# Seven block products for eight in the MLP of the last 1,024 tokens, taken together, with attention moved into the first two passes

## The chip, the cores and the metric

One core of one Trainium2 chip. Times are device microseconds of one execution; lower is better. The kernel runs in one launch and uses TensorE (PE), VectorE (DVE), ScalarE (ACT), GpSimd (POOL) and the DMA queue of SyncE (SP).

## The reference, cut to what matters

```python
h = h + concat([att, conv]) @ w_out            # att: dilated windows; conv: conformer
sc = (rmsnorm(h, norm_x_g) @ w_xq) . xk / 16   # cross-attention, 4 heads, 256 keys
h = h + (softmax(sc) . xv) @ w_xo
u = rmsnorm(h, norm_mlp_g) @ w_up              # 1024 -> 4096
h = h + square(relu(u)) @ w_down               # 4096 -> 1024
return rmsnorm(h, norm_final_g)                # 2,048 tokens, width 1,024, float32
```

## The kernel before

The activations lie transposed: a tile is 128 channels by 512 tokens, and width 1,024 is eight such tiles (`KC` = 8). Every large product is made of three matmuls (`mm3`, L197 to L200), since each operand is split into a high part and what the high part leaves over: weight high x activation high (L198), weight high x activation low (L199), weight low x activation high (L200). A weight tile comes as a raw 512 KB tile by a DMA from SP, ACT casts the high part (L189) and DVE subtracts it for the low part (L190); both are in `wsplit2`, and `wpost` (L1088) loads and splits a tile for the passes below.

The first 700 us or so make the queries, keys and values, the first block's attention and the convolution's input. Then come four passes, `post(p)` (L1217), each of 512 tokens: the output projection (tiles `o`, weights `raw_o`), scores and softmax of the cross-attention (`xs`, weights `raw_a`), its projection (`x`, weights `raw_b`), each with a residual and a sum of squares in `resid_linear` (L1194), then the norm's factor for each token, `rsb`, and the MLP. The MLP has eight groups (`fg`) of 512 hidden channels: four times 24 matmuls into one bank (`up`, weights `raw_u`), then relu times `rsb` (L1306), square (L1307), and the split into `hh` high (L1308) and low (L1309); then eight times 12 matmuls (`dn`, weights `raw_d`), each added to the residual `h` by DVE (L1324). So the up product works on activations without `rsb`, which comes in behind it at L1306. At the end the final norm and 16 transposed tiles of rows (`ot`, L1352 to L1356) go out. In the last pass the down products of the last group and the final norm are done for 256 tokens at a time.

The attention and the convolution of block p+1 run beside pass p. They are generators which `weave` (L92) advances by a rate each time the pass yields; what is left is drained at the end of the pass:

```python
sides = [(att(p + 1), 0.95), (conv(cv, p + 1), 0.6)] if p + 1 < NG else []
weave(main, *sides)
drain(*(g for g, _ in sides))
```

The last pass has nothing beside it. The order in which an engine gets its instructions is set by the order of these generators and by a scheduler that moves instructions of one engine past each other when it builds the program; tiles of one tag share a ring of buffers (`bufs`), and a load into a buffer waits for the last reader of what it held before.

Of the kernel before, what the change touches and what calls it, by code (L numbers as in the profile page):

```python
# [10 lines left out]
F32 = mybir.dt.float32  # L11
# [32 lines left out]
def f(ap):  # L44
    return ap.bitcast(F32)


def hybrid_layer(ctx, tc, A, out):
# [722 lines left out]
    early.close()  # L771


    kq = pool("att_keys", side="right")
    aq = pool("att_q", side="right")
    mask = pool("mask", side="right").tile([P, 6 * 256 + P], F32, name="mask")
    dma(mask, A["masks"])
    wk = pool("att_work", side="right")
    wk.tile([P, 144], F32, name="wpad")


# [356 lines left out]


    banks.update(mm=(0, 1, 2), O=(7,))  # L1140
    wq = pool("w_post", side="right")
    xp_ = pool("post_x")
    zp = pool("post_z")
    yp = pool("post_y")
    pp = pool("post")
    cv = pool("conv")
# [4 lines left out]
    def xquad(q, i, name):  # L1151
        return xp_.tile([P, 4, 512], F32R, tag=f"x{q}{i}", name=name)
# [22 lines left out]
        rstd_col(r[:, 0:n], pc[:, 0:n], n, top)  # L1175
        return r

    def load_cat(p, half):

        d = cats.setdefault(p, {})  # L1180
        for q in "hl":
            t = xquad(q, half, f"cat{q}{p}{half}")
# [11 lines left out]
    def resid_linear(load, rhs, korder, resid, hs, ssum, key, y, name, steps=False):  # L1194


        for ms in ((0, 1, 2), (3,), (4,), (5,), (6,), (7,)):
            wt = [load(m) for m in ms]
            pts = {}
            for ks in (korder[0:4], korder[4:6], korder[6:8]) if len(ms) > 1 else (korder,):  # L1200
                for m, (wh, wl) in zip(ms, wt):
                    if m not in pts:
                        pts[m] = ps("mm", f"{name}{m}")
                    for k in ks:
                        mm3(pts[m], wh[:, k, :], wl[:, k, :], rhs["h", k], rhs["l", k], k == korder[0], k == korder[-1])
                    if steps and ks[-1] != korder[-1]:
                        yield
                    if ks[-1] == korder[-1]:
                        h = hs[m]
                        last["dve"] = DVE.tensor_tensor(h, pts[m], resid(m), op=ALU.add)  # L1210
                        ACT.activation(y["h", m], h, AF.Copy, scale=gain(key, m))
                        DVE.scalar_tensor_tensor(y["l", m], h, gain(key, m), f(y["h", m]), op0=ALU.mult,
                                                 op1=ALU.subtract)
                        add_sq(h, ssum, m == 0)
                        yield

    def post(p):  # L1217
        ts = slice(512 * p, 512 * (p + 1))
        if p == 0:
            load_cat(0, 0)  # L1220
            load_cat(0, 1)
        hs = [zp.tile([P, 512], F32, tag=f"z{m}", name=f"h{p}_{m}") for m in range(KC)]

        def ytiles(name):
            return {(q, k): ytile(q, k, f"{name}{q}{p}_{k}") for k in range(KC) for q in "hl"}

        def from_x(m):
            x = tmp("res")
            dma(x, xscr[m][:, ts])
            return x  # L1230

        y = ytiles("y")
        ssum = ssum_tile(f"o{p}")
        yield from resid_linear(lambda m: wout[m] if p == 0 and m in wout else wpost(wcols(w_out, m * P), f"o{p}{m}"),
                                cats[p], [4, 5, 6, 7, 0, 1, 2, 3], from_x, hs, ssum, "x", y, f"o{p}_",
# [43 lines left out]
                        yield  # L1279
                yield  # L1280

        y = ytiles("m")
# [5 lines left out]
        rsb = ssum  # L1288
        ACT.copy(rsb, rb)


        FG = 8
        end = p == NG - 1
        for fg in range(FG):
            hh = {}
            for q in "hl":
# [13 lines left out]
                yield  # L1310
            if fg == FG - 1:
                fsum = ssum_tile(f"f{p}")
                if not end:
                    load_cat(p + 1, 0)

            def down(mp2, t, w, wh, wl):
                sl = slice(t, t + w)
                for e in range(2):
                    m = 2 * mp2 + e
                    es = slice(P * e, P * e + P)  # L1320
                    pt = ps("mm", "dn")[:, 0:w]
                    for k in range(4):
                        mm3(pt, wh[:, k, es], wl[:, k, es], hh["h", k][:, sl], hh["l", k][:, sl], k == 0, k == 3)
                    last["dve"] = DVE.tensor_tensor(hs[m][:, sl], hs[m][:, sl], pt, op=ALU.add)  # L1324
                    if fg == FG - 1:
                        add_sq(hs[m][:, sl], fsum[:, sl], m == 0)

            wd = []
            for mp2 in range(4):
                wd.append(wpost(wcols(w_down, mp2 * 256, 256, (4 * fg, 4 * fg + 4)), f"d{p}{fg}_{mp2}", (P, 4, 256)))  # L1330
                if fg == FG - 1 and end:
                    continue
                down(mp2, 0, 512, *wd[-1])
                yield


        fin = {}

        def final(t, w):
            r = rstd_from(fsum[:, t:t + w])  # L1340
            sl = slice(t, t + w)
            for k in range(KC):
                if t == 0:
                    fin[k] = ytile("h", k, f"fin{p}_{k}", F32)
                DVE.tensor_scalar(fin[k][:, sl], hs[k][:, sl], gain("final", k), None, op0=ALU.mult)
            for j in range(w // P):
                c0 = t + P * j
                for g in range(2):
                    ot = ytile("l", 2 * (c0 // P) + g, f"ot{p}{c0}{g}", F32)
                    pt = ps("T", "ot")  # L1350
                    for i in range(4):
                        PE.transpose(pt[:, P * i:P * i + P], fin[4 * g + i][:, c0:c0 + P], ident)  # L1352
                    if g:
                        ACT.activation(ot, pt, AF.Copy, scale=r[:, j:j + 1])
                    else:
                        DVE.tensor_scalar(ot, pt, r[:, j:j + 1], None, op0=ALU.mult)  # L1356
                    dma(out[0, 512 * p + c0:512 * p + c0 + P, 512 * g:512 * (g + 1)], ot)
                yield

        if end:  # L1360
            for t in range(0, 512, 256):
                for mp2 in range(4):
                    down(mp2, t, 256, *wd[mp2])
                yield from final(t, 256)
        else:
# [12 lines left out]

def _constants():
# [55 lines left out]
```

## Time and profile before

| | |
|---|---|
| three timed runs | 2896.39, 2896.18, 2894.63 us |
| median | 2896.18 us |
| the profiled execution | 2900.79 us, of it 2899.0 between the first and the last instruction |
| mean granted TensorE clock | 0.989 |
| matmul instructions on PE | 15,628 |
| moved by DMA | 433.73 MB |

In the profile's lines an instruction is named by its line, engine, operation and tiles (out<-in, buffer numbers left out). The windows give, for each stretch, the busy time of each engine with the number of instructions, then the granted clock of TensorE, the share of the 16 DMA engines that was busy, and GB/s. Pieces of the chain of waits are: start, duration, what. Pass 1 starts at some 1300 us, pass 2 at 1850, pass 3 at 2400, and the MLP of pass 3 at 2541.

### The profile page before, as it was taken

The numbers are of one execution on the slowest core, as the hardware profiler recorded it, in microseconds if no ns is written. First come the engines' busy times: TensorE is split into PE (matmuls) and PEld (weight loads), VectorE is DVE, ScalarE is ACT, GpSimd is POOL, SyncE is SP. The second block draws the span as 40 slices with busy tenths as digits, with TensorE's granted clock in tenths as the row PEclk, the third lists the DMA queues.
The fourth block names the chain that finished last, engine by engine and source line by source line (L and its number), as shares of the span: only waits on it lengthen the run. The fifth ranks groups of instructions, "written<-read, shape, count | busy, mean of one in ns | idle before, by whom it ended". The sixth has DMA issues, their size and how long they took to land.

```text
span 2899.0 us, 41416 instructions
## 1 busy us (share of the span) xinstructions
PE 2833.0 (98%) x15628; PEld 2386.6 (82%) x15628; DVE 1855.6 (64%) x3311; ACT 1171.3 (40%) x1988; POOL 474.0 (16%) x522
## 2 busy tenths in 40 slices
PE   8999999989999999999999999999999999999999
PEld 8878899878778888888788888887888888888888
DVE  6636535556789876557988655688876555644445
ACT  6633211556445334435443343444433433432233
POOL 1346321232002111200112120002011200000000
PEclk9999999999999999999999999999999999999999
DMA  8989745799644453554444454534443445233332
GB/s 271 312 170 237 186 115 150 192 245 244 184 117 128 126 145 115 163 156 147 118 139 125 130 158 151 177 105 122 133 136 97 141 126 177 87 95 98 98 95 73
DMA packets 606655, 433.73 MB, mean 150 GB/s; under 512 B 174885, under 2 KB 537433, under 8 KB 606456
## 3 DMA queue, kind: packets, MB, share of 16 engines
q1 hardware_dynamic: 566904, 408.81, 48.8%
q10 hardware_dynamic: 37952, 16.88, 2.2%
q0 software_dynamic: 1600, 5.41, 0.7%
q8 instruction: 123, 2.02, 0.3%
q14 instruction: 76, 0.62, 0.1%
HBM read 339.89 MB, written 91.11 MB: 149 GB/s over the span
## 4 chain that ended last, share of the span: by engine, by line
PE 87%; DMA 5%; DVE 3%; ACT 2%; issue 1%; SPq 1%; POOL 0%; ACTq 0%; POOLq 0%; DVEq 0%
PE dn L198 8%; PE dn L199 8%; PE dn L200 8%; PE up L198 8%; PE up L200 8%; PE up L199 8%; PE lin L198 4%; PE lin L200 4%; PE lin L199 4%; PE o L198 2%; PE pt L792 2%; PE o L199 2%; PE o L200 2%; PE x L198 2%; PE x L200 2%; PE x L199 2%
## 5 line engine op out<-in xcount | busy, mean ns | idle before, releaser
L199 PE MATMUL dn<-hhl,whi_d 128*128 128x512 f32 (+1 forms) x1056 | 402.2, 384 | 1.6 <-DVE hhl L1309 1.6
L198 PE MATMUL up<-mh,whi_u 128*128 128x512 f32 x1024 | 401.9, 393 | 1.2 <-DVE rl L1306 1.2
L200 PE MATMUL dn<-hhh,wlo_d 128*128 128x512 f32 (+1 forms) x1056 | 401.1, 384 | 0.0
L200 PE MATMUL up<-mh,wlo_u 128*128 128x512 f32 x1024 | 399.9, 391 | 0.0
L198 PE MATMUL dn<-hhh,whi_d 128*128 128x512 f32 (+1 forms) x1056 | 398.4, 390 | 0.7 <-DVE h L1324 0.6
L199 PE MATMUL up<-ml,whi_u 128*128 128x512 f32 x1024 | 398.6, 389 | 0.0
L215 DVE SCALAR_TENSOR_TENSOR cacc<-cu,cw,cacc 128x512 f32<-128x512 f32 x480 | 386.9, 808 | 4.9
L1324 DVE TENSOR_TENSOR h<-h,dn 128x512 f32<-128x512 f32 (+1 forms) x264 | 172.9, 669 | 240.6 <-PE dn L200 239.6
L189 ACT CAST whi_u<-raw_u 128x1024 fp32r<-128x1024 f32 x128 | 134.6, 1052 | 437.3 <-PE dn L199 402.4
L189 ACT CAST whi_d<-raw_d 128x1024 fp32r<-128x1024 f32 x128 | 134.2, 1051 | 349.4 <-PE up L199 314.2
L198 PEld LDWEIGHTS dn<-hhh,whi_d 128*128 128x128 f32 x1056 | 197.8, 188 | 41.7 <-DVE h L1324 5.2
L200 PEld LDWEIGHTS dn<-hhh,wlo_d 128*128 128x128 f32 x1056 | 198.4, 188 | 39.2
L1306 DVE SCALAR_TENSOR_TENSOR rl<-up,ssumx 128x512 f32<-128x512 f32 x128 | 87.9, 690 | 222.2 <-PE up L200 218.7
L199 PEld LDWEIGHTS dn<-hhl,whi_d 128*128 128x128 f32 x1056 | 198.7, 188 | 38.1 <-DVE hhl L1309 2.5
L200 PEld LDWEIGHTS up<-mh,wlo_u 128*128 128x128 f32 x1024 | 192.2, 188 | 40.7
L198 PEld LDWEIGHTS up<-mh,whi_u 128*128 128x128 f32 x1024 | 192.2, 188 | 40.0 <-DVE rl L1306 2.0
L199 PEld LDWEIGHTS up<-ml,whi_u 128*128 128x128 f32 x1024 | 192.3, 188 | 38.5
L786 ACT ACTIVATE sm<-sm,o 128x256 f32<-128x256 f32 (+1 forms) x384 | 160.9, 466 | 132.3 <-DVE o L785 132.2
L190 DVE TENSOR_TENSOR wlo_d<-raw_d,whi_d 128x1024 fp32r<-128x1024 f32 x128 | 157.8, 1233 | 30.4 <-ACT whi_d L189 30.0
L785 DVE CUSTOM_DVE_ANT_0 sm<-s,mask 128x256 f32<-128x256 f32 (+1 forms) x384 | 128.4, 375 | 64.0 <-PE s L1005 37.6
L190 DVE TENSOR_TENSOR wlo_u<-raw_u,whi_u 128x1024 fp32r<-128x1024 f32 x128 | 159.0, 1242 | 9.6 <-ACT whi_u L189 8.9
L176 POOL TENSOR_TENSOR nr<-st_v,mhalf 128x4 f32<-128x4 f32 (+1 forms) x13 | 14.0, 1077 | 897.9 <-DVE st_v L172 897.9
(402 smaller groups left out, 6361.8 us busy)
## 6 DMA issues: line engine op xcount, KB each, us to landing
raw_u<-in_w_up_dram SPq DMA_DIRECT2D x128, 512.0 KB
raw_d<-in_w_down_dram SPq DMA_DIRECT2D x128, 512.0 KB
raw_o<-in_w_out_dram SPq DMA_DIRECT2D x32, 512.0 KB
raw_a<-ascr SPq DMA_DIRECT2D x32, 512.0 KB
raw_b<-bscr SPq DMA_DIRECT2D x32, 512.0 KB
v<-vtok SPq DMA_DIRECT2D x208, 65.0 KB
k<-kscr SPq DMA_DIRECT2D x24, 512.0 KB
k<-kscr SPq DMA_DIRECT2D x8, 1152.0 KB
```

The costliest lines, as they stand in the source:

```text
L176: POOL.tensor_tensor(dst, v, mhalf.to_broadcast([P, v.shape[1]]), op=ALU.pow)
L189: ACT.copy(hi, raw)
L190: (lo_eng or DVE).tensor_tensor(lo, raw, f(hi), op=ALU.subtract)
L198: PE.matmul(o, lh, rh, start=first, stop=False)
L199: PE.matmul(o, lh, rl, start=False, stop=False)
L200: last["pe"] = PE.matmul(o, ll, rh, start=False, stop=end)
L215: DVE.scalar_tensor_tensor(acc, u[:, t:t + 512], cw[:, c, t:t + 1], acc, op0=ALU.mult, op1=ALU.add)
L785: last["dve"] = DVE.tensor_tensor_reduce(dst, so, mask[:, 256 * m:256 * m + nk], 1.0, 3e38, ALU.add, ALU.min, mn)
L786: last["act"] = ACT.activation(dst, dst, AF.Exp, bias=mn, scale=-1.0)
L792: last["pe"] = PE.transpose(pt[:, j, :], sm[:, j, :], ident)
L1306: last["dve"] = DVE.scalar_tensor_tensor(r, pt, 0.0, rsb, op0=ALU.max, op1=ALU.mult)
L1324: last["dve"] = DVE.tensor_tensor(hs[m][:, sl], hs[m][:, sl], pt, op=ALU.add)
```

## The change

Passes 0 and 1 stay as they are, but carry the attention and the convolution of blocks 1, 2 and 3, one behind the other, at rates 1.31 and 0.84. `until` runs a side forward to the block that is needed next. Passes 2 and 3 end ahead of the MLP (`before_mlp`): their residuals go to memory (`hscr`), and `rsb` is multiplied in ahead of the up product.

The MLP of these two passes is one, over 1,024 tokens, by block products. The inner width of 1,024 and the tokens are halved, the hidden channels taken in pairs of 128-blocks, 16 apart; each 2x2 block product takes seven products of blocks instead of eight, with sums of blocks made beforehand, of activations (`b11`, `b21`, `b22`, and `t1` to `t4`, split once) and of weights (`s12`, `s34`, by DVE in each step). A product of blocks is 12 matmuls (`prod`). In the up half two of the seven (`plain_half`, with `b11` and `b21`, into one bank) need only raw weights; three such pairs are taken in advance (`PRO`), and each of the 16 steps of `up_pairs` has the other five, 60 matmuls, and from the fourth on a plain half of 24. The results are squared; seven blocks of each step (256 KB each) go to memory (`rscr`), four of them sums made by POOL and DVE. The raw weights of a step are two tiles of 512 KB, `raw_um` and `raw_ub`, in one ring of two buffers.

The down half is four sweeps over the 16 steps, `p`, `q` and `r` with two of the seven products each (24 matmuls a step into eight banks in all) and `s` with one. Each reads its blocks back from memory and loads rows of w_down; sums of weights are kept in `keep`. Between the sweeps the banks are added to the residuals (`HD_`), read back from memory, by DVE and POOL. The final norm of pass 2's tokens follows sweep `r`, that of pass 3's tokens sweep `s`, both for 512 tokens at a time.

The core of the diff:

```diff
+    BLK = ("b11", "b21", "b22", "t1", "t2", "t3", "t4")
+    rscr = {(b, k): dr.tile([P, 512], F32, name=f"r{b}_{k}") for b in BLK for k in range(DFF // 256)}
+    hscr = {(p, k): dr.tile([P, 512], F32, name=f"hs{p}_{k}") for p in (2, 3) for k in range(KC)}
+    yscr = [dr.tile([P, 512], F32, name=f"ys{k}") for k in range(KC)]
...
+    def before_mlp(p, hs, hook=None):
         ts = slice(512 * p, 512 * (p + 1))
...
+        y = ytiles("m", p) if p < 2 else None
...
+        rsb = ssum if p < 2 else rsbs[p]
         ACT.copy(rsb, rb)
-
-
-        FG = 8
-        end = p == NG - 1
+        return y, rsb
...
+    FG = 8
+
+    def post(p):
+        if p == 0:
+            load_cat(0, 0)
+            load_cat(0, 1)
+        hs = [zp.tile([P, 512], F32, tag=f"z{m}", name=f"h{p}_{m}") for m in range(KC)]
+        y, rsb = yield from before_mlp(p, hs)
...
-        if end:
-            for t in range(0, 512, 256):
-                for mp2 in range(4):
-                    down(mp2, t, 256, *wd[mp2])
-                yield from final(t, 256)
-        else:
-            load_cat(p + 1, 1)
-            yield from final(0, 512)
...
-    for p in range(NG):
...
+    class Chain:
+        def __init__(self, make):
+            self.done = 0
+            self.gen = self.steps(make)
+
+        def steps(self, make):
+            for p in range(1, NG):
+                yield from make(p)
+                self.done = p
+
+    def until(c, p):
+        while c.done < p:
+            if next(c.gen, c) is c:
+                break
+
+    atts, convs = Chain(att), Chain(lambda p: conv(cv, p))
+    sides = [(atts.gen, 1.31), (convs.gen, 0.84)]
+    for p in range(2):
...
-        sides = [(att(p + 1), 0.95), (conv(cv, p + 1), 0.6)] if p + 1 < NG else []
         weave(main, *sides)
-        drain(*(g for g, _ in sides))
...
+    def after_scores():
+        until(convs, 3)
+        until(atts, 3)
+        conv_st.close()
+        attn.close()
...
+    weave(before_mlp(2, h2, after_scores), *sides)
...
+    for k in range(KC):
+        dma(hscr[2, k], h2[k])
+        yn = tmp("yn")
+        DVE.scalar_tensor_tensor(yn, h2[k], gain("mlp", k), rsbs[2], op0=ALU.mult, op1=ALU.mult)
+        dma(yscr[k], yn)
+        split_to("b21" if k > 3 else "b11", k % 4, yn)
+    banks.update(mm=(0, 1, 2, 7))
...
+    drain(before_mlp(3, h3, swap_late))
...
+    for k in range(4):
+        n = [yt_(f"yn3_{k}{i}") for i in range(2)]
+        for i in range(2):
+            kk = 4 * i + k
+            DVE.scalar_tensor_tensor(n[i], h3[kk], gain("mlp", kk), rsbs[3], op0=ALU.mult, op1=ALU.mult)
+            dma(hscr[3, kk], h3[kk])
+        split_to("b22", k, n[1])
+        t1b, t2b = yt_(f"yt1_{k}"), yt_(f"yt2_{k}")
+        DVE.tensor_tensor(t1b, n[0], yn2[k], op=ALU.subtract)
+        DVE.tensor_tensor(t2b, n[1], t1b, op=ALU.subtract)
+        split_to("t2", k, t2b)
+        late_tile("t1", k)
+        split_to("t1", k, t1b)
+        t3b = yt_(f"yt3_{k}")
+        POOL.tensor_tensor(t3b, n[1], n[0], op=ALU.subtract)
+        split_to("t3", k, t3b)
+        t4b = yt_(f"yt4_{k}")
+        POOL.tensor_tensor(t4b, yn2[4 + k], t2b, op=ALU.subtract)
+        late_tile("t4", k)
+        split_to("t4", k, t4b)
...
+    def prod(o, w, b, first):
+        for k in range(4):
+            for x, (i, q) in enumerate(((0, "h"), (0, "l"), (1, "h"))):
+                PE.matmul(o, w[i][:, k, :], Y[b][q][k], start=first and k + x == 0, stop=k == 3 and x == 2,
+                          skip_group_check=not first)
...
+    def wraw(src, name):
+        raw = wp.tile([P, 8, P], F32, tag="raw", name=f"raw_{name}", bufs=2)
+        dma(raw, src)
+        return raw
...
+    PRO = 3
+    st1 = {}
+
+    def plain_half(i, raw=None):
+        raw = raw or wraw(wcols(w_up, i * P), f"ua{i}")
+        a11, a12 = halves(wpair(raw, f"ua{i}"))
+        b1 = ps("b1", f"b1_{i}")
+        prod(b1, a11, "b11", True)
+        c1 = wt_(f"c1_{i}")
+        ACT.copy(c1, b1)
+        yield
+        prod(b1, a12, "b21", False)
+        r11 = wt_(f"r11_{i}")
+        squared(r11, b1)
+        dma(rscr["b11", i], r11)
+        st1[i] = c1, r11
+        yield
+
+    def up_pairs():
+        prev = iter(())
+        for i in range(NP):
+            ra = wraw(wcols(w_up, i * P), f"um{i}")
+            ph = iter(()) if i < PRO else plain_half(i, ra)
+            next(ph, None)
+            rb_ = wraw(wcols(w_up, (i + 16) * P), f"ub{i}")
+            s12 = pm.tile([P, 8, P], F32, tag="s12", name=f"s12_{i}")
+            s34 = pm.tile([P, 8, P], F32, tag="s34", name=f"s34_{i}")
+            DVE.tensor_tensor(s12[:, 0:4], rb_[:, 0:4], rb_[:, 4:8], op=ALU.add)
+            DVE.tensor_tensor(s12[:, 4:8], s12[:, 0:4], ra[:, 0:4], op=ALU.subtract)
+            a5, a6 = halves(wpair(s12, f"us{i}"))
+            DVE.tensor_tensor(s34[:, 0:4], ra[:, 0:4], rb_[:, 0:4], op=ALU.subtract)
+            DVE.tensor_tensor(s34[:, 4:8], ra[:, 4:8], s12[:, 4:8], op=ALU.subtract)
+            a7, a3 = halves(wpair(s34, f"ut{i}"))
+            n = turn_w[0]
+            turn_w[0] += 1
+            a4 = wsplit2(wq if n % 4 > 1 else wp, rb_[:, 4:8], f"uu{i}", shape=(P, 4, P))
+            b2 = ps("b2", f"b2_{i}")
+            b3 = ps("b3", f"b3_{i}")
+            prod(b2, a6, "t2", True)
+            next(prev, None)
+            next(ph, None)
+            c1, r11 = st1[i]
+            u2, u3 = yt_(f"u2_{i}"), yt_(f"u3_{i}")
+            DVE.tensor_tensor(u2, b2, c1, op=ALU.add)
+            prod(b3, a5, "t1", True)
+            prod(b2, a7, "t3", False)
+            DVE.tensor_tensor(u3, b2, c1, op=ALU.add)
+
+            def rest(i=i, a3=a3, a4=a4, b2=b2, b3=b3, u2=u2, u3=u3, c1=c1, r11=r11):
+                r22, r21, r12 = (zp.tile([P, 512], F32, tag=f"z{3 * (i % 2) + x}", name=f"r{i}_{x}") for x in range(3))
+                DVE.tensor_tensor(r22, b3, u3, op=ALU.add)
+                squared(r22, r22)
+                dma(rscr["b22", i], r22)
+                prod(b2, a4, "t4", False)
+                DVE.tensor_tensor(r21, b2, c1, op=ALU.add)
+                squared(r21, r21)
+                dma(rscr["b21", i], r21)
+                prod(b3, a3, "b22", False)
+                DVE.tensor_tensor(r12, b3, u2, op=ALU.add)
+                squared(r12, r12)
+                T = [r12, yt_(f"rt{i}1"), zp.tile([P, 512], F32, tag=f"z{6 + i % 2}", name=f"rt{i}2"), yt_(f"rt{i}3")]
+                POOL.tensor_tensor(T[2], r22, r12, op=ALU.subtract)
+                DVE.tensor_tensor(T[0], r12, r11, op=ALU.subtract)
+                DVE.tensor_tensor(T[1], r22, T[0], op=ALU.subtract)
+                DVE.tensor_tensor(T[3], r21, T[1], op=ALU.subtract)
+                for x in range(4):
+                    dma(rscr[f"t{x + 1}", i], T[x])
+                yield
+
+            prev = rest()
+        next(prev, None)
+
+    for i in range(PRO):
+        drain(plain_half(i))
+    up_pairs()
...
+    keep = [hp_.tile([P, 512], F32, tag=f"s{k}", name=f"keep{k}") for k in range(NP)]
+    HD_ = {p: [(zp if p == 3 else hp_).tile([P, 512], F32, tag=f"z{k}" if p == 3 else f"h2{k}", name=f"hd{p}_{k}")
+             for k in range(KC)] for p in (2, 3)}
+    for k in range(KC):
+        for p in (2, 3):
+            dma(HD_[p][k], hscr[p, k])
...
+    def sweep(tag, blocks, weights, kinds):
+        acc = []
+        for k in range(NP):
+            n = len(blocks)
+            braw = bp.tile([P, n, 512], F32, tag="braw", name=f"braw_{tag}{k}", bufs=3)
+            bh = bp.tile([P, n, 512], F32R, tag="bh", name=f"bh_{tag}{k}", bufs=3)
+            bl = bp.tile([P, n, 512], F32R, tag="bl", name=f"bl_{tag}{k}", bufs=3)
+            for i, b in enumerate(blocks):
+                dma(braw[:, i], rscr[b, k])
+            wh, wl = wsplits(f"{tag}{k}", weights(k))
+            ACT.copy(bh, braw)
+            DVE.tensor_tensor(bl, braw, f(bh), op=ALU.subtract)
+            for i in range(n):
+                if k == 0:
+                    acc.append([ps(kinds[i], f"{tag}{i}{m}") for m in range(4)])
+                for m in range(4):
+                    ms = slice(P * m, P * m + P)
+                    mm3_at(acc[i][m], wh[:, i, ms], wl[:, i, ms], bh[:, i], bl[:, i], k == 0, k == NP - 1)
+        return acc
...
+    def w_first(k):
+        raw = wp.tile([P, 2, 512], F32, tag="raw", name=f"raw_da{k}", bufs=2)
+        dma(raw, w_rows(k).rearrange("p (x m) -> p x m", x=2))
+        DVE.tensor_tensor(keep[k], raw[:, 0], raw[:, 1], op=ALU.subtract)
+        return [raw[:, 0], keep[k]]
...
+    def w_third(k):
+        raw = wp.tile([P, 2, 512], F32, tag="raw", name=f"raw_dc{k}", bufs=2)
+        r12 = wd_.tile([P, 512], F32, tag="ra", name=f"raw_dd{k}", bufs=3)
+        dma(r12, w_rows(k + NP, 0))
+        dma(raw[:, 0], w_rows(k, 1))
+        dma(raw[:, 1], w_rows(k + NP, 1))
+        DVE.tensor_tensor(raw[:, 0], raw[:, 0], raw[:, 1], op=ALU.add)
+        DVE.tensor_tensor(keep[k], r12, keep[k], op=ALU.subtract)
+        return [r12, raw[:, 0]]
...
+    m1, m7 = sweep("p", ("b11", "t3"), w_first, "XY")
+    for m in range(4):
+        e, t = e_tile(f"e1{m}"), e_tile(f"e7{m}")
+        ACT.copy(e, m1[m])
+        DVE.tensor_tensor(t, m7[m], e, op=ALU.add)
+        plus(HD_[2][m], e, POOL)
+        plus(HD_[3][m], e, POOL)
+        plus(HD_[2][4 + m], t, POOL)
+        plus(HD_[3][4 + m], t, POOL)
...
+    m4, m6 = sweep("q", ("t4", "t2"), w_second, "XY")
...
+    m2, m5 = sweep("r", ("b21", "t1"), w_third, "XY")
...
+    (m3,) = sweep("s", ("b22",), lambda k: [keep[k]], "X")
...
+    for m in range(KC):
+        sq(2, m, m == 0)
+        closing(2, m)
+    drain(rows(2))
+    for m in range(4, 8):
+        sq(3, m, m == 4)
+        closing(3, m)
+    for m in range(4):
+        plus(HD_[3][m], m3[m], DVE)
+        sq(3, m, False)
+        closing(3, m)
+    drain(rows(3))
```

More of the change, by code (lines that the diff above doesn't have):

```diff
@@ L1280, in post @@
                 yield
-        y = ytiles("m")
+        if hook:
+            hook()
+        y = ytiles("m", p) if p < 2 else None
         ssum = ssum_tile(f"x{p}")
@@ L1312, in post @@
                 fsum = ssum_tile(f"f{p}")
[L1313 to L1317, printed above, removed]
+                until(convs, p + 1)
+                load_cat(p + 1, 0)
+            for mp2 in range(4):
+                wh, wl = wpost(wcols(w_down, mp2 * 256, 256, (4 * fg, 4 * fg + 4)), f"d{p}{fg}_{mp2}", (P, 4, 256))
                 for e in range(2):
@@ new lines, in hybrid_layer @@
+    m1, m7 = sweep("p", ("b11", "t3"), w_first, "XY")
[9 more added lines that the diff above has]
+    for m in range(4):
+        e = e_tile(f"e6{m}")
+        plus(HD_[2][4 + m], m4[m], DVE)
+        ACT.copy(e, m6[m])
+        plus(HD_[3][m], e, POOL)
+        plus(HD_[2][4 + m], e, POOL)
+        plus(HD_[3][4 + m], e, POOL)
@@ new lines, in hybrid_layer, with sq @@
+    m2, m5 = sweep("r", ("b21", "t1"), w_third, "XY")
+    sums = {p: e_tile(f"fs{p}") for p in (2, 3)}
+    def sq(p, k, first):
+        if first:
+            ACT.activation(sums[p], HD_[p][k], AF.Square)
+        else:
+            q = e_tile(f"sq{p}{k}")
+            ACT.activation(q, HD_[p][k], AF.Square)
+            DVE.tensor_tensor(sums[p], sums[p], q, op=ALU.add)
+    for m in range(4):
+        e = e_tile(f"e5{m}")
+        plus(HD_[2][m], m2[m], DVE)
+        ACT.copy(e, m5[m])
+        plus(HD_[3][m], e, POOL)
+        plus(HD_[3][4 + m], e, POOL)
```

189 lines of the change are left out of this document (135 added, 54 removed).

## Prediction

> **What bounds the kernel now.** The page's first part and its chain come first.
>
> ```profile
> PE 2833.0 (98%) x15628; PEld 2386.6 (82%) x15628; DVE 1855.6 (64%) x3311; ACT 1171.3 (40%) x1988; POOL 474.0 (16%) x522
> ...
> PE 87%; DMA 5%; DVE 3%; ACT 2%; issue 1%; SPq 1%; POOL 0%; ACTq 0%; POOLq 0%; DVEq 0%
> ```
>
> TensorE is busy 98% of the span and carries 87% of the chain that ends last, so its matmuls are the first suspects. A busy TensorE need not be a fast one; the chain in the last pass shows the pace. The same place of a group of the MLP comes up at even distances:
>
> ```profile
> 2563.42 0.68 PE dn L198 x3
> ...
> 2607.11 0.68 PE dn L198 x3
> ...
> 2650.80 0.68 PE dn L198 x3
> ```
>
> A group (96 matmuls up, 96 down) takes 43.69 us, so a fed 128x512 matmul is 43.69 / 192 = 0.2276 us. All four MLPs go at this pace. Next, the windows by stage (whole kernel passes 1 and 2, pass 3 ahead of its MLP, its MLP, and the inside of that):
>
> ```profile
> 1300.00:1850.00 550.00, 545.11 (x2882) 451.50 (x2880) 396.21 (x669) 228.64 (x363) 76.94 (x88) 0.99 0.46 138
> 1850.00:2400.00 550.00, 543.91 (x2863) 450.45 (x2861) 392.74 (x651) 226.16 (x357) 70.99 (x84) 0.99 0.44 131
> 2400.00:2541.00 141.00, 140.03 (x651) 115.45 (x651) 80.12 (x131) 59.67 (x101) 2.03 (x2) 1.00 0.39 125
> 2541.00:2899.00 358.00, 350.77 (x1651) 292.57 (x1649) 174.53 (x242) 109.54 (x145) 2.41 (x3) 0.99 0.29 92
> 2563.00:2869.00 306.00, 305.96 (x1367) 252.63 (x1366) 144.90 (x175) 92.37 (x115) 0.00 (x0) 1.00 0.30 93
> ```
>
> The columns are TensorE, weight loads, VectorE, ScalarE, GpSimd. The MLP of the last pass is the stage with most slack: in 306 us TensorE stops for 0.04 us, VectorE has 145, the DMA engines 0.30. So every matmul that goes there is worth its 0.2276 us, as long as what replaces it fits beside TensorE in time and in order.
>
> **Part 1, matmuls that go.** The MLP of 1,024 tokens is 16 groups of 192 = 3,072 matmuls. Afterwards: up, 16 steps of 84 (five products of 12, a plain half of 24) = 1,344; down, three sweeps of 384 and one of 192 = 1,344; together 2,688. That is 384 fewer: -87.4 us. The half-width products of the last group go too:
>
> ```profile
> 2887.14 0.28 PE L199 MATMUL dn<-hhl,whi_d 128*128 128x256 f32 x1
> ...
> 2888.33 0.28 PE L200 MATMUL dn<-hhh,wlo_d 128*128 128x256 f32 x1
> ```
>
> Between these two are nine more, ten steps in 1.19 us: 192 at 0.119 are 22.8 us, 96 whole ones 21.9: -0.9. Together **-88.3**.
>
> **Part 2, the up loop.** TensorE has 84 x 0.2276 = 19.1 us a step. The other engines' durations:
>
> ```profile
> L189 ACT CAST whi_u<-raw_u 128x1024 fp32r<-128x1024 f32 x128 | 134.6, 1052 | 437.3 <-PE dn L199 402.4 <-PE x L199 20.6 <-issue 13.5
> L1308 ACT CAST hhh<-rl 128x512 fp32r<-128x512 f32 x128 | 78.8, 618 | 2.9
> L190 DVE TENSOR_TENSOR wlo_u<-raw_u,whi_u 128x1024 fp32r<-128x1024 f32 x128 | 159.0, 1242 | 9.6 <-ACT whi_u L189 8.9
> L1306 DVE SCALAR_TENSOR_TENSOR rl<-up,ssumx 128x512 f32<-128x512 f32 x128 | 87.9, 690 | 222.2 <-PE up L200 218.7 <-ACT ssumx L1289 3.5
> L1324 DVE TENSOR_TENSOR h<-h,dn 128x512 f32<-128x512 f32 x248 | 166.3, 685 | 237.3 <-PE dn L200 236.7
> L944 POOL TENSOR_TENSOR cat<-cat,ld 128x512 f32<-128x512 f32 x30 | 42.2, 1407 | 1.2
> ```
>
> VectorE has 3 splits of 1024 columns and 13 operations of 512, some 12.6 us of 19.1: by totals the loop fits. By order it does not. Of the program's order I followed which instruction each wait of one step stands for. Both raw weights of a step lie in one ring of two buffers, so the second raw tile (`raw_ub`) of step i+1 is loaded into the buffer that step i's last split (`uu`) reads, and `uu` in turn waits for a weight slot that step i's last product (b22) holds. So, from the end of b22 of step i: the cast `whi_uu` 0.62 (beside it VectorE's `r12` add, to 0.85), `wlo_uu` 0.69 (to 1.55), the load of `raw_ub` with its latency L, then on VectorE in order `s12` first half, `s34` first half, `T1`, `s12` second half: 4 x 0.69 = 2.76, the cast `whi_us` 1.05: L + 5.35. Only then comes the next step's first product. Behind b22 TensorE has the rest of a plain half alone, 22 matmuls = 5.0 us. The pause is L + 0.35. For L there are these rows, the last load of each tile and the cast that waits for it, and a piece of the chain:
>
> ```profile
> L189 ACT CAST whi_b<-raw_b x6: 1035/1054/1056, 2481.0 to 2512.0; 128x1024 fp32r<-128x1024 f32 x6
> L57 SPq DMA_DIRECT2D raw_b<-bscr x4: 319/320/320, 2483.3 to 2508.6; - x4
> ...
> 729.64 5.99 DMA raw_o<-in_w_out_dram
> ```
>
> 3.4 us for 512 KB in long rows in a quiet stretch, 5.99 for 512 KB in rows of 512 bytes (as `raw_ub` has) in a crowded one. I take 4.5, between them: the rows are short, the stretch is quiet. The pause is then 4.85 (3.75 to 6.35). Were the load never late, GpSimd's `T[2]`, which stands ahead of `s12` on VectorE (b22, the add 0.85, two activations 1.24, 1.41 on GpSimd, `T0` 0.69, then the same 2.76 and 1.05), would leave 8.0 - 5.0 = 3.0. Twelve steps so, 58 us; the second and third steps, which have no plain half as cover, some 7 each: **+72** (52 to 89).
>
> The Trainium skill, "DMA: Bandwidth & Descriptors", section "Anatomy of one DMA", gives 2.0 us and the bytes at 436 GB/s for a transfer (its fit is for the other DMA path): an estimate of 3.2 us for 512 KB; the row of 5.99 differs, that of 3.4 agrees, and the up loop would cost 18 us less by it.
>
> **Part 3, the clock after a pause.** What a pause of that length does is in the windows at 750 us, where TensorE stood still for some 4 us:
>
> ```profile
> 745.00:750.00 5.00, 4.37 (x22) 1.00 0.92 259
> 750.00:755.00 5.00, 1.04 (x4) 0.78 0.86 227
> 755.00:760.00 5.00, 4.00 (x21) 0.50 0.70 160
> 760.00:765.00 5.00, 5.00 (x19) 0.70 0.15 46
> ```
>
> The granted clock falls to 0.50 and stays low for 6 to 8 us after work resumes: 0.5 x 4.0 + 0.3 x 5.0 = 3.5 us lost. Shorter pauses elsewhere (VectorE's waits under 1 us in the MLPs) leave it at 1.00. The pause of part 2 is split by a copy of `c1` and some 4.2 of it is in one piece, at the edge; I take half of the 14 pauses at 2.5 us, **+17** (0 to 49, at 3.5 each).
>
> The Trainium skill, "TensorE: Matmul & The Clock Gate", section "Part 1: The HAM clock gate", has a free-running window of about 3.4 us: one idle window halves the clock, one busy window restores it. A pause of 4.2 us would hold a whole window in a quarter of cases, at 1.7 us each: 6 us by it instead of 17. The trace agrees that the clock halves; its loss is twice as long.
>
> **Part 4, into the up loop.** In the kernel before, the norm of the tokens (`rsb`) is applied behind the up product, and TensorE goes on. Now it goes in ahead of the products: after `rsb` VectorE has 4 x (2 x 0.745 + 7 x 0.69) = 25.3 us plus the first weights' sums 3, with 0.745 the mean of the split with gain:
>
> ```profile
> L1212 DVE SCALAR_TENSOR_TENSOR yl<-h,gv,yh 128x512 fp32r<-128x512 f32 x32 | 23.4, 745 | 0.0
> ```
>
> TensorE has the three plain halves and 12 matmuls of cover, 84 x 0.2276 = 19.1; some 3 more go in the norm's own chain of four engines: **+12** (5 to 20).
>
> **Part 5, up to down.** Eight tiles `hd2` and eight `hd3` (16 x 262 KB = 4.2 MB) are loaded ahead of the third rows of w_down on SP's queue, and `hd3` waits for buffers of the up loop's last results. At the peak rate
>
> ```profile
> 80.00:120.00 40.00, 39.97 (x294) 1.00 0.98 323
> ```
>
> that is 13 us, after which come 0.5 MB of blocks and 0.5 MB of weights for each 5.46 us of TensorE, a hundred and ninety GB/s: **+12** (5 to 20).
>
> **Part 6, the sweeps.** Step k of a sweep has 24 x 0.2276 = 5.46 us. In `p` the raw rows of step k+2 are loaded behind the first split of step k, and VectorE takes `keep` of k+2 ahead of the splits of k+1: L + 2 x 0.69 = 5.9 at 4.5, so 16 x 0.4 = 7 at most, taken as **+4** (0 to 8). In `r` the two halves of `raw_dc` of step k+2 are loaded behind both splits of k, and the sum of k+2 again stands ahead of the splits of k+1: an issue 0.4, L, the sum and two splits 3 x 0.69. The loads are of 256 KB; at L = 3.9, between 3.4 and 4.5, this is 6.4, so 16 x 0.9 = **+14** (4 to 24). `q` moves half as much: 0. Three changes of sweep, where banks are emptied by four or eight operations of 0.69 ahead of the next first product: **+5** (4 to 8).
>
> **Part 7, the end.** Before, the last product is done in halves of 256 columns and ends at 2888.6, the second row of part 1; the span ends 10.4 us later:
>
> ```profile
> 2895.11 0.75 DVE ot L1356
> ...
> L1345 DVE TENSOR_SCALAR fin<-h,gv 128x512 f32<-128x512 f32 x24 | 11.3, 482 | 0.2
> ```
>
> Now four whole adds, four sums and four gains (4 x (0.69 + 0.69 + 0.48) = 7.4) stand behind the last product, and twice the rows to turn and write: **+9** (6 to 10).
>
> **Part 8, passes 0 and 1.** Pass 2 against pass 3 without attention is 393 against 255 us of VectorE, so a token block's attention and convolution is 138. At one and a half of these, VectorE has 255 + 207 = 462 of about 575 us. In the densest stretch of before
>
> ```profile
> 1476.00:1520.00 44.00, 43.76 (x256) 36.07 (x255) 39.35 (x71) 20.28 (x34) 3.08 (x2) 1.00 0.48 140
> ```
>
> TensorE lost 0.24 of 44 us with VectorE at 89%, so 80% on average costs little: **+5** (0 to 25).
>
> **The sum.** -88.3 + 72 + 17 + 12 + 12 + 4 + 14 + 5 + 9 + 5 = +61.7. On the profiled execution (2900.79, its span 2899.0) that is 2962.5; the median of the three runs is 2896.18, 4.6 lower, so 2957.9: **2958 us**. With every low end: -88.3 + 52 + 0 + 5 + 5 + 0 + 4 + 4 + 6 + 0 = -12.3, 2884; all high ends together (89 + 49 + 20 + 20 + 8 + 24 + 8 + 10 + 25 - 88.3 = +165) are not likely, and half of the way from the sum to them is 3010.
>
> **Rivals.**
> *Faster: the loads land early.* With L = 3.4 the pause is 3.75, of which 3.1 is in one piece, too short for the clock; the rest costs its low ends: the -12.3 above, 2884. If only GpSimd's chain holds the loop (3.0 a step), 14 x 0.75 less, 2874; if TensorE had no pause at all in the loop, 2832. For it: the quiet share of 0.30 in the MLP. Against: the order of part 2, in which even a load without delay leaves 3.0, and 2.75 MB a step where the MLP before had 1 MB in 10.9 us. It decides from L below about 3.6. Chance 0.24.
> *Slower still: the clock stays low.* With L = 6 the pause is 6.35 and each one halves the clock: 89 + 49 instead of 72 + 17: +111, 3007; with `r` at 24 as well, 3017. For it: the row of 750 us. Against: that row is from a stage with DMA at 0.86. Chance 0.10.
> *The dense passes:* attention at 1.5 times the pace makes VectorE late for the MLP's products by the 25 us of part 8: 2978. For it: 89% at the peak before. Against: order is laid out by the same rates through both passes. Chance 0.08.
>
> **How the numbers follow.** My forecast has 0.55, the rivals 0.24, 0.10 and 0.08, about no change (the lower waits and the gain in balance) 0.03. The range, 2864 to 3012, leaves out a tenth at each end. The two ends of the range stand between the rivals' bounds: the lower under GpSimd's 2874, the upper between 3007 and 3017. A change under 0.2% (6 us) can't be told from none here. Faster 0.24, within 0.2% 0.03, slower 0.73.
>
> **What would show it.** Right: in the up loop a step takes about 24 to 26 us instead of 19.1; the wait at the first product of each step is for `whi_us`, whose chain goes through `wlo_uu` and the DMA of `raw_ub`; the granted clock there is between 0.8 and 0.95; the wait in the third sweep is on `raw_dc`. Wrong: steps of 19 to 20 us at a clock of 1.00, with the total near 2860; or a loss that lies ahead of the joint MLP.

## The result, and the profile after

The changed kernel takes 3042.74 us (median of 4 runs, 3042.07 to 3046.82) for 2896.04 before: a ratio of 1.051, 95% interval 1.0492 to 1.0529. It is slower, as forecast, but by 147 us and not by 62; it lies above the range.

The first part of the page after, its columns as before:

```profile
PE 2817.6 (93%) x15148; PEld 2348.1 (77%) x15148; DVE 1985.4 (65%) x3448; ACT 1239.0 (41%) x2132; POOL 555.3 (18%) x581
```

TensorE has 480 instructions fewer, yet is busy only 15 us less, and its share of the span fell from 98% to 93%. The windows of TensorE by stage after the change (length, busy, granted clock, DMA share, GB/s) tell where:

```profile
740.00:960.00 220.00, 196.40 (x1145) 0.92 0.49 141
960.00:1386.00 426.00, 415.18 (x2343) 0.99 0.51 148
1386.00:1966.00 580.00, 562.03 (x3048) 0.99 0.50 147
1966.00:2256.00 290.00, 277.09 (x1273) 0.98 0.43 138
2256.00:2664.00 408.00, 336.01 (x1287) 0.89 0.33 113
2664.00:2780.00 116.00, 100.80 (x419) 0.93 0.65 211
2780.00:2868.00 88.00, 87.66 (x387) 1.00 0.51 159
2868.00:2967.00 99.00, 90.92 (x385) 0.98 0.53 169
2967.00:3041.00 74.00, 60.87 (x276) 0.89 0.28 97
```

The rows are: pass 0 ahead of its MLP; its MLP; pass 1; passes 2 and 3 ahead of theirs; the up loop; the sweeps `p`, `q`, `r`; `s` with the end. Three kinds of stage lose. In the up loop TensorE stands still for 72 us, at a mean granted clock of 0.89. The sweeps `p` and `r` and the end lose 10 to 30 us each. And the passes 0 and 1, which the change only gave more attention, lose before any new product is reached: the row at 740 us has 24 us of idle time and a clock of 0.92, where the same stage had 10 us and 0.96 before.

### The profile page after: what moved, and what is told of

It reads as the page before. It is cut to its first block, busy times and chain, and to the rows that moved or that the text cites. A ratio compares the mean times of both kernels' runs of the same rounds, so it can differ in the third digit from the quotient of the medians.

```text
span 3040.9 us, 41375 instructions
## 1 busy us (share of the span) xinstructions
PE 2817.6 (93%) x15148; PEld 2348.1 (77%) x15148; DVE 1985.4 (65%) x3448; ACT 1239.0 (41%) x2132; POOL 555.3 (18%) x581
## 5 line engine op out<-in xcount | busy, mean ns | idle before, releaser
L202 PE MATMUL up<-mh,whi_u 128*128 128x512 f32 x512 | 202.1, 396 | 0.0
L203 PE MATMUL dn<-hhl,whi_d 128*128 128x512 f32 x512 | 200.5, 393 | 0.1
L203 PE MATMUL up<-ml,whi_u 128*128 128x512 f32 x512 | 200.4, 392 | 0.0
L204 PE MATMUL up<-mh,wlo_u 128*128 128x512 f32 x512 | 200.4, 392 | 0.0
L202 PE MATMUL dn<-hhh,whi_d 128*128 128x512 f32 x512 | 198.6, 399 | 1.3 <-DVE h L1335 1.3
L204 PE MATMUL dn<-hhh,wlo_d 128*128 128x512 f32 x512 | 199.4, 392 | 0.0
L801 DVE TENSOR_TENSOR pl<-pt,ph 128x512 f16<-128x512 f32 x160 | 108.6, 683 | 41.0 <-ACT ph L800 40.2
L202 PE MATMUL o<-cath,whi_o 128*128 128x512 f32 x256 | 104.0, 408 | 12.7 <-DVE h L1217 11.9
L797 PE MATMUL pt<-ident,sm 128*128 128x128 f32 x640 | 105.2, 285 | 7.8 <-ACT sm L791 4.0
L204 PEld LDWEIGHTS dn<-hhh,wlo_d 128*128 128x128 f32 x512 | 96.5, 188 | 20.3
```

The costliest lines, as they stand in the source:

```text
L202: PE.matmul(o, lh, rh, start=first, stop=False)
L203: PE.matmul(o, lh, rl, start=False, stop=False)
L204: last["pe"] = PE.matmul(o, ll, rh, start=False, stop=end)
L797: last["pe"] = PE.transpose(pt[:, j, :], sm[:, j, :], ident)
L801: DVE.tensor_tensor(pl, pt, ph, op=ALU.subtract)
```

## The experiments

All times are medians beside runs of the kernel before on the same chip (2896 to 2900 us), with the ratio and its interval. The theories: the up loop and the sweeps lose by the waits that the prediction lists; for the passes 0 and 1, density (more attention on VectorE and ScalarE than they can carry beside TensorE) against order (the change also moves the pool `w_post` to the other side of the memory, and so the order that the scheduler lays out).

### Attention in the first two passes, all else as before

```diff
-        sides = [(att(p + 1), 0.95), (conv(cv, p + 1), 0.6)] if p + 1 < NG else []
+    sides = [(atts.gen, 1.31), (convs.gen, 0.84)]   # Chain and until as in the change
```

> The kernel before, with the MLP of every pass as it was (eight products), but with the attention and the convolution of blocks 1 to 3 run in a chain beside passes 0 and 1 at the rates 1.31 and 0.84. After the change the last sum of squares of pass 1 is at 1965.6 us for some 1850 before; 52 us of that is attention that is moved and would only be saved later, some 64 are lost. If the density itself costs them (VectorE and ScalarE late for TensorE), this kernel loses the same: 2896 + 64 = 2960 us, and its first sum of squares of pass 0's second norm comes well behind before's 915. If they come from another order of the engines that has nothing to do with the rates (the pool of the weights, w_post, stands on another side of the memory), this kernel is at 2896 to 2915.

2947.12 us, 1.0171 (1.0153 to 1.0189): +49.4 us. The rows of the second and third norms, whose first start is in pass 0; before had 915.3 and 1297.6:

```profile
L1173 PE MATMUL nps<-ones,ssumx x32: 164/250/250, 942.4 to 2587.0; 128*128 128x1 f32 x32
L1173 PE MATMUL nps<-ones,ssumf x32: 164/250/271, 1370.4 to 2935.7; 128*128 128x1 f32 x32
```

Part of these delays is attention that now comes earlier, and no loss. What follows pass 1 is 58 us shorter than before (2943.8 - 1952.1 = 991.7 us for 2899.0 - 1849.3 = 1049.7, the ends of pass 1 being its last norm's): that is the attention that was moved. Pass 1 ends 102.8 us later, so 45 us are lost there. Most of the loss in the changed kernel, though not all, comes with the density.

### One pool on the other side

```diff
-    wq = pool("w_post", side="right")
+    wq = pool("w_post")
```

> The kernel before with one word changed: the pool of the passes' split weights, w_post, is allocated from the left like the others and not from the right. All work and all rates stay. If the order of the engines that follows from the pools costs the passes 0 and 1 their time, the stretch up to pass 0's second norm grows as after the change (915 to 940 or 960 us) and the kernel is 25 to 60 us slower: 2920 to 2956. If density is the cause, it is at 2896, give or take 5.

2917.53 us, 1.0066 (1.0046 to 1.0085): +19.8 us from one word, with all work and all rates as before. ScalarE's timeline shows one place where it is lost, first in the kernel before, then in this one, then after the change:

```profile
721.09 1.05 ACT L189 CAST whi_o<-raw_o 128x1024 fp32r<-128x1024 f32 x1 [1.68 <-DMA catl<-catl]
```

```profile
711.23 1.04 ACT L189 CAST whi_o<-raw_o 128x1024 fp32r<-128x1024 f32 x1 [8.08 <-DMA raw_o<-in_w_out_dram]
```

```profile
715.86 1.04 ACT L193 CAST whi_o<-raw_o 128x1024 fp32r<-128x1024 f32 x1 [8.64 <-DMA raw_o<-in_w_out_dram]
```

The bracket is the idle time ahead of the instruction and what ended it. Before, the load of these weights is issued at 701.75 and their cast stands behind attention's own casts (`ph`), 19 us later. In the other two kernels the order has the cast in front of those. That this is because the split weights now lie where buffers are free earlier is argued and not shown. The load takes longer than this order allows for (after the change 9.8 us from its issue at 706.02 to the cast), ScalarE waits in order, and behind it TensorE, for 8.00 us in this kernel and, after the change, for 8.56:

```profile
717.44 0.24 PE L805 MATMUL opt<-v,ph 128*128 128x65 f16 x1 [8.56 <-ACT ph L800]
```

Neither theory is the whole. At the end of pass 1 the first kernel has lost 45 us and this one 14 (1863.6 for 1849.3; the one wait above is 8 us). The changed kernel has lost 58 there (1965.6 for 1849.3, less the 58 that are moved): the two add up. In the medians of the whole kernels they are 49 and 20.

### The same attention, placed within the MLPs

```diff
-    sides = [(atts.gen, 1.31), (convs.gen, 0.84)]
+    sides = [(atts.gen, (0.7, 1.35)), (convs.gen, (0.45, 0.87))]   # ahead of an MLP, within it
```

> As the kernel of eight products with attention in passes 0 and 1 (2947 us), but with two rates for each side: 0.7 and 0.45 ahead of an MLP, where VectorE is busy at 83% already, and 1.35 and 0.87 within it, where it is at some 50%. If the density costs where VectorE has no slack, ahead of the MLPs, the loss of 49 us falls to 10 to 25 and the second norm of pass 0 comes at about 920 us for 942. If attention costs the same wherever it is put, the total stays at 2940 to 2950.

2897.66 us, 0.9995 (0.9985 to 1.0004): the 49 us are gone altogether. All three blocks' attention still lies in passes 0 and 1 (its last product starts at 1864.0, pass 1's last norm at 1899.4), but pass 0's second norm comes at 901.9 and its third at 1320.5:

```profile
L1175 PE MATMUL nps<-ones,ssumx x32: 164/250/250, 901.9 to 2535.4; 128*128 128x1 f32 x32
L1175 PE MATMUL nps<-ones,ssumf x32: 164/250/272, 1320.5 to 2884.0; 128*128 128x1 f32 x32
```

So it is not the amount of attention in a pass that costs, but how densely it is laid ahead of the MLP, beside cross-attention and the output projection. The windows of 60 us near the end of that stage in pass 0 show the difference, in the kernel before, in the first experiment and in this one (the columns as in the prediction):

```profile
845.00:905.00 60.00, 56.23 (x325) 46.53 (x324) 55.23 (x107) 31.67 (x61) 14.43 (x18) 0.97 0.42 117
845.00:905.00 60.00, 51.45 (x318) 42.41 (x317) 56.23 (x118) 30.68 (x62) 16.46 (x20) 0.89 0.42 125
845.00:905.00 60.00, 59.15 (x315) 48.73 (x314) 49.71 (x85) 27.11 (x46) 3.08 (x3) 1.00 0.43 125
```

With VectorE at 56 us TensorE stands still for 8.6, with VectorE at 50 for 0.9. But VectorE's share alone does not decide it: before, with VectorE at 55 us, TensorE stood still for 3.8, and in the MLP of pass 0 VectorE is at 83% in both experiments (355 of 428 us and 350 of 419), while TensorE stands still for 12 us in the first and for 2 in this one. GpSimd's work in the windows above fell too, from 16 to 3 us, and the longest of TensorE's waits there in the first experiment (2.5 us) ends behind a cast of ScalarE that had itself waited 4.4 us for a load. No run separates these. That the rate ahead of the MLPs is the cause is shown; through which engine it acts is not.

### Lower rates in the changed kernel

```diff
-    sides = [(atts.gen, 1.31), (convs.gen, 0.84)]
+    sides = [(atts.gen, 1.08), (convs.gen, 0.69)]
```

> The changed kernel with the rates 1.08 and 0.69 for 1.31 and 0.84: attention ends 930 matmuls later, still ahead of pass 2's scores, and is spread more evenly over the passes 0 and 1, ahead of the MLPs and within them. If density is what costs the passes 0 and 1 (49 of the 65 us), 10 to 20 us come back: 3022 to 3032. If only the order from the pools counts there, nothing: 3038 to 3046.

3026.64 us, 1.0447 (1.0427 to 1.0468): 16 us back. Pass 1's last norm comes at 1947.8 for 1965.6, in part because the end of attention (its last product starts at 1980.1) now lies behind it. It agrees with the last experiment.

### Another buffer for the up loop's last split

```diff
     def wpair(t, name):
-        n = turn_w[0]
-        turn_w[0] += 1
-        return wsplit2(wq if n % 4 > 1 else wp, t, name)
+        return wsplit2(wq if name[1] == "s" else wp, t, name)
...
-            a4 = wsplit2(wq if n % 4 > 1 else wp, rb_[:, 4:8], f"uu{i}", shape=(P, 4, P))
+            a4 = wsplit2(wq, rb_[:, 4:8], f"uu{i}", shape=(P, 4, P))
```

First what this is aimed at, one step of the up loop in the changed kernel's timeline (start, duration, engine, instruction, and in brackets the wait ahead of it):

```profile
2459.85 0.63 ACT L193 CAST whi_uu<-raw_ub 128x512 fp32r<-128x512 f32 x1 [0.47 <-PE b L1477]
...
2460.68 0.68 DVE L194 TENSOR_TENSOR wlo_uu<-raw_ub,whi_uu 128x512 fp32r<-128x512 f32 x1
...
2461.39 0.38 SPq L57 DMA_DIRECT2D raw_ub<-in_w_up_dram  x1
...
2465.14 0.69 DVE L1525 TENSOR_TENSOR s<-raw_ub 128x512 f32<-128x512 f32 x1 [0.92 <-DMA raw_ub<-in_w_up_dram]
2465.75 0.68 DVE L1528 TENSOR_TENSOR s<-raw_um,raw_ub 128x512 f32<-128x512 f32 x1
...
2467.68 1.04 ACT L193 CAST whi_us<-s 128x1024 fp32r<-128x1024 f32 x1 [0.38 <-DVE s L1526]
```

```profile
PE b L1477 <- ACT whi_us L193: 39.0, 11, 6.3
PE b L1477 <- DVE u L1541: 14.2, 5, 3.3
PE b L1477 <- ACT c L1507: 8.1, 12, 0.7
PE b L1477 <- DVE Yt2l L1410: 5.7, 3, 4.5
```

The second fence is TensorE's waits in the up loop (us in all, times, longest). The chain is the one of the prediction, link by link: the last product releases `uu`, its split releases the buffer, the load takes 3.75 us, four sums later (one of them for a result) `whi_us` is made. In this step TensorE's pause ends with `u` (L1541), a sum that stands behind those four in VectorE's order, 0.1 us after `whi_us`:

```profile
2468.90 0.80 PE L1477 MATMUL b<-Yt3h,whi_ut 128*128 128x512 f32 x1 [2.90 <-DVE u L1541]
```

> The changed kernel with the split weights of the up loop put in other buffers: the sums us and the raw half uu share one pair of buffers, ua and ut the other. So the split uu of a step waits for the product of us of that step and no more for the last product, b22, of the step before, and the load of raw_ub behind it starts some 10 us earlier. If the load of raw_ub behind b22 is what holds TensorE, the up loop goes from 407 us to about 330 (306 of matmuls, the transition ahead of it, no pause long enough for the clock), the total from 3042.7 to about 2967. If VectorE's order or GpSimd's subtraction holds it, a pause of 3 us a step stays and the total falls by 15 at most.

2972.06 us, 1.0254 (1.0239 to 1.0269): -70.7 us. Its up loop, and the transition ahead of it:

```profile
2259.00:2596.00 337.00, 307.46 (x1290) 0.95 0.41 136
```

337 us for 408. The load of `raw_ub` behind the last product was what held TensorE; neither VectorE's total nor GpSimd's subtraction did. Of the 30 us in which TensorE still stands idle, 25 come ahead of 2360 us, at the loop's start, 14 of them in waits for the operands (`Yt2`, `Yt1`).

### The residuals' loads from another queue

```diff
-            dma(HD_[p][k], hscr[p, k])
+            dma(HD_[p][k], hscr[p, k], POOL)
```

> The changed kernel with the 16 loads of the residuals (hd) issued from GpSimd's queue and not from SP's. Sweep p takes 116 us for 87.4 of matmuls. If the rows of w_down are late because they stand behind these loads on SP's queue, the sweep goes to about 100 us and the total down by 12 to 18, to 3026. If the bytes themselves fill the DMA engines at that place, the total stays within 5 us of 3042.7.

3039.70 us, 1.0489 (1.0463 to 1.0514): -3 us in the median, less than expected and not clear of the scatter (four runs from 3033.07 to 3044.78). SP's timeline after the change, and the wait of TensorE there, in the changed kernel and then in this one:

```profile
2689.18 6.61 SPq L57 DMA_DIRECT2D hd<-hs  x11
2696.14 0.96 SPq L57 DMA_DIRECT2D raw_da<-in_w_down_dram  x2
...
2702.46 0.79 PE L202 MATMUL p<-bh_p,whi_p 128*128 128x512 f32 x1 [5.23 <-ACT whi_p L1604]
```

```profile
2696.14 0.50 PE L202 MATMUL p<-bh_p,whi_p 128*128 128x512 f32 x1 [0.43 <-ACT whi_p L1604]
```

The one wait that the queue caused is gone. Sweep `p` starts at 2662.7 and ends at 2772.2, 109.5 us for 116, but its two earlier pauses stay, and of the 6.5 us the median shows 3.

### Putting the edits together

The first kernel takes the last two edits and allocates the pool of the residuals ahead of `w_post`.

> The changed kernel with three edits: the up loop's split weights in the other buffers (-70.7 alone), the loads of hd from GpSimd (-3 alone), and the pool of the residuals allocated ahead of w_post's, so that w_post lies elsewhere than after the change but not where it was before. If the edits add up and the place makes no difference, 2969; if the place brings the order of before back, 15 us less, 2954; if another order is worse, up to 2990.

2968.54 us, 1.0242 (1.0227 to 1.0257): -74 us, as the two edits alone gave together; that place of the pool changes nothing. The next adds the two rates:

> As the kernel with the three edits, with the two rates 0.7 and 0.45 ahead of an MLP and 1.35 and 0.87 within it. If density ahead of the MLPs is the cost, 25 to 40 us under that one: 2930 to 2945. If not, the same as that one.

2920.51 us, 1.0080 (1.0057 to 1.0102): -48 us, as much as the whole loss of the first experiment. The next puts `w_post` back on the right side:

```diff
+    wqs = [pool("w_post", stack=wst, side="right")]
...
+        wst.close()
         attn.close()
+        wqs.append(pool("w_post2", side="right"))
```

> The kernel of the two rates (2920.5 us) with the pool w_post back on the right side of the memory in passes 0 to 2 and opened anew there for the rest, and the pool of the residuals where it was. If the place of that pool costs what the kernel before lost by it alone (20 us of 2897), and the order of the first block's attention comes back with it, 2900 to 2910. If that loss was of an order of its own that has gone with the other edits, 2915 to 2925.

2909.46 us, 1.0039 (1.0024 to 1.0054): -11 us, some half of what the word cost alone. The next goes at four waits:

```diff
-        yn = tmp("yn")
+        yn = ynq[:, k % 4]      # two quads of post_x, free at that point
...
-        DVE.tensor_tensor(keep[k], raw[:, 0], raw[:, 1], op=ALU.subtract)
+        POOL.tensor_tensor(keep[k], raw[:, 0], raw[:, 1], op=ALU.subtract)
...
-        DVE.tensor_tensor(raw[:, 0], raw[:, 0], raw[:, 1], op=ALU.add)
+        POOL.tensor_tensor(raw[:, 0], raw[:, 0], raw[:, 1], op=ALU.add)
...
+            if tag == "s" and k >= NP - 3:
+                ends.append((wh, wl, bh, bl))    # multiplied bank by bank behind the loop
+                continue
```

and the operands `t4` and `b22` in a loop of their own behind `t1`, `t2` and `t3`.

> The last kernel with four more edits, each at a wait that its trace shows: the normalised activations of pass 2 in other buffers than the residual loads of pass 3 (11.8 us at the change of pass), the operands t1, t2, t3 made ahead of t4 and b22 (12 us and the clock behind it ahead of the up loop), the sums of raw weights in sweeps p and r on GpSimd (10 us of waits in r), and the last three steps of sweep s bank by bank (10 us of the end). If each wait gives back half to two thirds of itself, 20 to 30 us under the last kernel: 2875 to 2890, which is faster than before. If these waits only make room for the next ones, 2895 to 2905.

2895.38 us, 0.9985 (0.9974 to 0.9995), short of what was expected. In sweep `p` TensorE's waits were

```profile
PE p L204 <- ACT whi_p L1613: 15.7, 2, 13.7
```

since the sums that I had moved to GpSimd stood behind the issues of `hd` that I had moved there too. The last kernel takes those of sweep `p` back to VectorE.

> The last kernel with the sums of raw weights of sweep p back on VectorE; those of sweep r stay on GpSimd. In the last kernel sweep p had one pause of 13.7 us, where GpSimd's first sums stood behind the 16 issues of the hd loads on the same engine, and took 119 us; with VectorE's sums it took 109. If that queue is the cause, 8 to 12 us less: 2884 to 2888, faster than before by some 0.4%. If the rows of w_down themselves are late there, nothing: 2893 to 2897.

2877.36 us (median of 6), 0.9935 (0.9921 to 0.9949): faster than the kernel before by 0.65%, and by 165 us than the change as it came. It is 18 us under the last kernel (14 by the ratios), more than expected; sweep `p` itself went from 119 to 108, and the rest was not traced. The two windows of its up loop's start and its rest:

```profile
2184.00:2240.00 56.00, 35.68 (x105) 0.70 0.21 61
2240.00:2507.00 267.00, 261.83 (x1131) 1.00 0.44 150
```

The up loop runs at the pace of the matmuls and at full clock; its start, where the operands are made behind the norm, still loses some 30 us (35.68 us busy at a clock of 0.70 is 25 of 56). Of the 88 us of matmuls that the block products save, about 20 arrive.

## Why the prediction was wrong in size

- **Part 1, matmuls, -88.3:** the counts hold. Sweep `q`, the one stage without pauses, takes 87.8 us for 384 matmuls (87.4).
- **Parts 2, 3 and 4, the up loop, its clock and its start, +72 +17 +12 = +101:** 408 us for 306 of matmuls, +102. That the sums agree to 1 us is luck, since two errors cancel. The pauses of the twelve full steps were shorter than my 4.85 us, 2.9 to 3.3 and the 0.7 of the copy, since L was 3.75 and VectorE's sums follow each other at 0.60, not 0.69; the second and third steps paused 6.3 and 6.0 us for my 7, and the start took 14 for my 12. The clock was worse:

```profile
2465.00:2470.00 5.00, 2.10 (x8) 0.81 0.59 225
2470.00:2475.00 5.00, 5.00 (x14) 0.51 0.37 107
...
2490.00:2495.00 5.00, 2.00 (x9) 1.00 0.59 213
2495.00:2500.00 5.00, 4.78 (x14) 0.66 0.65 210
```

  336 us busy for 306 is some 30 us by the clock where I took 17, and idle time was 72 for my 84. My bound that 3.1 us in one piece are too short for the clock was wrong: 2.9 us ahead of 2468.9 were enough. The Trainium skill's "DMA: Bandwidth & Descriptors", section "Anatomy of one DMA", gave an estimate of 3.2 us for L, by a fit for the other DMA path; 3.75 is nearer to it than to my 4.5.
- **Parts 5 and 6, the sweeps:** `p` +29 for +16 (12 and 4): mis-sized. SP's order was one of three pauses; the others are the last step of the up loop, with no plain half left as cover, and the first rows. `r` +11.7 for +14, which is near in part by luck: of TensorE's 8.1 us of waits there, 4.8 fall in the first 22 us, where VectorE's sums and splits of 512 columns took 1.7 to 1.8 us instead of 0.7 while GpSimd added to the residuals. Only the other 3.3 come where VectorE waits for the loads of `raw_dc` and `raw_dd`, the cause that I had named. `s` +8.9 for +5.
- **Part 7, the end, +9:** from `s`'s last matmul at 3020.3 to 3040.9 it is 20.6 for 10.4, +10.
- **Part 8, the passes 0 and 1, +5 (0 to 25):** +58. This is the step that failed, and alone more than half of the 85 us between forecast and result. I took the density of a whole pass (80% of VectorE) against one stretch of 44 us at 89% that lost nothing, and that stretch lay in an MLP. Ahead of its MLP, in pass 0 without the change, VectorE was already at 157 of 190 us and TensorE stood still for 10:

```profile
725.00:915.00 190.00, 179.83 (x1017) 148.39 (x1018) 157.10 (x305) 85.58 (x158) 27.92 (x29) 0.96 0.49 141
```

  There the rate went up by 38%. The denser attention is 45 of the 58 us, and the two rates give them back. The other 14, the order that follows from the place of a pool, were not in the sum at all, though the full diff has that line.
- **Not in the sum:** passes 2 and 3 ahead of their MLP take 290 us for 282. One wait of 11.9 us, where pass 3's residual loads share four buffers with the normalised tiles of pass 2, makes more than all of that. With those tiles elsewhere, in the kernel that goes at four waits, it is 0.7.

```profile
PE o L202 <- DVE h L1217: 11.9, 1, 11.9
```

The measured parts sum to -88 + 102 + 29 + 12 + 9 + 10 + 58 + 8 = +140, for 3040.9 - 2899.0 = 141.9 of spans. Of the rivals, the dense passes were the true one beside the forecast, priced at 25 us in all, where the passes lost 58 and the density alone 45; I had given them 0.08 and as an alternative to the forecast, where they came in addition. The signs that I had named for the up loop came: a step takes 25.6 us, the clock is 0.9, and the waits go through `raw_ub`. So did one that I had named for being wrong, a loss that lies ahead of the joint MLP.

## What to carry to other kernels

When work moves beside other work, compare the engines stage by stage, not pass by pass: the same attention cost 49 us at one rate and nothing at two, of which the lower stood ahead of the MLPs. A load that waits for a buffer, which waits for a split, which waits for the last product of a step, is a loop through the whole machine; one other choice of buffer gave back 71 us. And a diff that moves a pool moves the order of instructions far from it.

## What the hardware showed that I had not expected

A pause of TensorE of 2.9 us, with a shorter one of 0.68 and twelve matmuls ahead of it, was followed by a granted clock of 0.51 in the window of the next 5 us. In the up loop twelve pauses of 2.9 to 3.3 us and two of some 6 make 50 of its 72 us of idle time; the clock took some 30 more, the loop's start included. Two VectorE sums of 128x512 that follow each other start 0.61 us apart (2465.14 and 2465.75) though each is recorded with 0.68 or 0.69: a chain of four is 2.5 us and not 2.76. While GpSimd added to the residuals behind sweep `q`, VectorE's sums and splits of 512 columns took 1.7 to 1.8 us, from 2871.7 to 2888.7 us, and 0.68 behind that; no run here tests whether the one causes the other.
